# Attention of a two-layer decoder trunk: token-major projections and softmax over merged key columns, blocks outermost, in one written order with both channel mixers

## The chip, the cores and the metric

One core of a Trainium2 chip runs the whole program. The metric is the device time of one execution in microseconds, the median of several runs.

## The reference

Input x is 1024 tokens of 1024 float32 features. Layer 0 mixes tokens by a short gated convolution, layer 1 by attention; each is followed by a SwiGLU channel mixer (hidden width 2816). RMSNorm stands ahead of each of the four, a residual around it. The attention has 16 query heads of 64, 4 key/value heads, a window of 128 keys in blocks of 128 queries:

```python
q = rmsnorm(q, q_gain); k = rmsnorm(k, k_gain)          # per head of 64
scores = einsum('bnqkgd,bnskd->bnkgqs', qb, kw) * scale  # kw: previous and own block, 256 keys
dist = qi + BLOCK - kj
mask = (dist >= 0) & (dist < WINDOW) & (key_pos >= 0)
scores = where(mask, scores - slopes * dist, -inf)
p = softmax(concat([scores, sink_col]))[..., :-1]
out = einsum('bnkgqs,bnskd->bnqkgd', p, vw)
return out.reshape(bsz, s, 1024) @ w_o
```

Since the window equals the block, query i of a block sees the keys j <= i of its own block and j > i of the one before: each of the 128 columns is live in exactly one of the two.

## The kernel before, in words

Activations lie feature-major: eight tiles X of 128 features by 1024 tokens. Every product is made of three matmuls on numbers split into an upper and a lower part of fp32r (w.hi x.hi, w.hi x.lo, w.lo x.hi). The big products of the mixers use a seven-product scheme in place of eight; granule_work (L922 to L935) issues their matmuls. A class Line (L780) holds an order: work(n, f) appends TensorE work and advances a clock of planned time, at(t, f) hangs other engines' work on that clock, and run() emits all in the order of planned time under a manual schedule. The clock only sets each queue's order; on the chip every engine runs its own queue, waiting on semaphores.

The convolution layer and its channel mixer (channel_mixer, L990) are one Line, run at its end. Then attention_layer (L1524) begins anew. Keys and queries are projected with the weights stationary, so they come out feature-major, two heads to a tile (project_k L1609, the loop over i from 1 to 7 with product_by_halves L186); values are projected with tokens stationary, 256 columns at a time (project_v L1583). Sums of squares per head are matmuls with two columns (head_stats, L1536 to L1539); the inverse roots are spread to 64 columns each, transposed on TensorE and multiplied in (spread, turn_blocks L1624 to L1627, scale_rows). The softmax works on units of a tile i of two heads and a block b, 64 in all, tiles outermost. A unit's scores are four matmuls of 256 keys (scores, L1743 to L1753); VectorE adds the distance bias and finds the extreme (maxima, L1774), ScalarE exponentiates with sums (exponents, L1792), a column is blanked (blank, L1796), the weights are transposed by 128 x 128 (turn, L1798 to L1804), split (turn_hi L1811, turn_lo L1817) and multiplied with the values by up to four matmuls of 256 columns (values, L1819 to L1830). Division by the sums follows later (divide_steps, L1849), again over spread and transposed rows. A string ORDER sets the order of the steps inside a unit, and an agenda the rest:

```python
ORDER = "SPTZMEDkPHLBVOPK"
```

The output projection is split: the products over tiles 0 to 3 (L192) are threaded through the last units, those over tiles 4 to 7 are the head of the second channel mixer, which is a Line of its own (tail_part L1045, tail_item L1064, L1058 to L1060), its weights kept for both halves of the tokens. The first gate-up products come after it. SP issues the loads, GpSimd some stores.

Of the kernel before, what the change touches and what calls it, by code (L numbers as in the profile page):

```python
# [31 lines left out]
TILES = [0, 2, 1, 3, 4, 6, 5, 7]  # L32
HEADS = [2 * i + e for i in TILES for e in range(2)]
SLOPES = [2.0 ** (-8.0 * (h + 1) / NH) for h in HEADS]

# [6 lines left out]
C_INVS = C_KG + 1  # L42
C_NEGS = C_INVS + NH
C_ONES = C_NEGS + NH
C_HALF = C_ONES + 1
C_ID = C_HALF + 2
C_DIST = C_ID + P
C_END = C_DIST + 2 * P


LAG = 10

ORDER = "SPTZMEDkPHLBVOPK"


EARLY = 4
REST = 2
# [24 lines left out]
def trunk_kernel(ctx: ExitStack, tc: tile.TileContext, xT, small, w_in, w_out, w_qk, w_v, w_o, w_gu, w_dn, out):  # L82
# [136 lines left out]
    for tag in [f"G{k}" for k in range(12)]:  # L219
        slot(tag)  # L220
# [6 lines left out]
    half = cst[:, C_HALF : C_HALF + 2]  # L227
    dist = cst[:, C_DIST : C_DIST + 2 * P]

# [91 lines left out]
    def conv_layer():  # L321
# [410 lines left out]
        def lead_in(part):  # L732
# [19 lines left out]
        channel_mixer(  # L752
# [6 lines left out]
            keep_tags=None,  # L759
# [11 lines left out]
        )  # L771


    xres = [tc.dram_tile((P, T), F32, name=f"xres{m}") for m in range(NK)]
    first_sums = [[tc.dram_tile((4, P, 4 * P), F32, name=f"s1_{l}_{u}") for u in range(GROUP)] for l in range(2)]
# [214 lines left out]
    def channel_mixer(layer, next_stage, src_of, operands, raw_tags, extra_tags, keep_tags, slots, begin_with=(), first_w=None, line=None, lead_in=None):  # L990

        line = line or Line()
        at = line.at
        for t, f in begin_with:
            at(t, f)
        n_op = len(operands)
# [9 lines left out]
        kept = {}  # L1006

        def tail_weights(h, m, t):
            it = {}
            c = slice(0, n_op * P)  # L1010
            if keep_tags is None:

                def load():
                    it["w"] = Weights()
                    it["w"].load(src_of(m), 0, n_op)

                def hi():
                    it["w"].alloc()
                    it["steps"] = split_steps(it["w"].hi[:, c], it["w"].lo[:, c], it["w"].raw[:, c])
                    it["steps"][0]()  # L1020

                at(t - 14.0, load)
                at(t - 5.2, hi)
                at(t - 4.2, lambda: it["steps"][1]())
                return lambda: (it["w"].hi, it["w"].lo)
            if h == 0 and m in (first_w or ()):
                kept[m] = first_w[m]
            elif h == 0:

                def load():  # L1030
                    raw = slot("WR", (P, n_op * P), bufs=2)
                    nc.sync.dma_start(raw.rearrange("p (k c) -> p k c", c=P), src_of(m))
                    it["raw"] = raw

                at(t - 9.0, load)
                split_granule(it, lambda: it["raw"], n_op, keep_rooms[m], t - 4.0)
                kept[m] = it
            it = kept[m]
            return lambda: (it["w"][:, 0], it["w"][:, 1])

        keep_rooms = rooms(keep_tags) if keep_tags else None
# [3 lines left out]
        def tail_part(h, m, ks):  # L1045

            c = slice(h * HALF, h * HALF + HALF)
            if (h, m) not in tails:
                tails[h, m] = tail_weights(h, m, line.end), bank_at(("tail", h, m), "x", "acc")
# [14 lines left out]
        def tail_item(h, m, k0=0):  # L1064
# [5 lines left out]
            def square():  # L1070
                if m == 0:
                    state["ss", h] = slot(f"s{h}", (P, HALF))
# [47 lines left out]
        if lead_in is not None:  # L1120
            first_items = lead_in(tail_part)
# [43 lines left out]
        if not whole:  # L1165
            at(origin + 8 * tail * 0.65, load_s2)
# [1004 lines left out]
```

## Time and profile before

| | |
|---|---|
| three runs | 1949.97, 1949.94, 1949.57 us, median 1949.94 |
| profiled execution, span from first to last instruction | 1948.8 us |
| TensorE busy in it | 1937.3 us, 99% |
| VectorE, ScalarE, GpSimd busy | 71%, 44%, 13% |
| instructions | 25694 |

The time of the profiled execution is known by its span alone; what lies around it is taken as the 1.1 us between span and median. Busy shares are of the whole span; the rows below go to the stretches. A matmul's mean duration is latency in a pipeline and not its pace.

### The profile page before, as it was taken

What the parts mean: (1) busy time and instruction counts of PE and PEld (TensorE: products, weight loads), DVE (VectorE), ACT (ScalarE), POOL (GpSimd) and SP (SyncE); (2) the same over time, 40 slices, a digit from 0 to 9 for tenths busy, and PEclk for the clock granted to TensorE, in tenths of its full rate; (3) what the DMA queues carried; (4) which work ended last, traced back from release to release, by engine and by line L of the source; (5) the groups of instructions that cost most, each with busy time, mean ns of one, the idle gap of its engine ahead of it and who ended that gap; (6) DMA issues with size and microseconds to landing.
All of it is one profiled execution on the core that took longest, in us unless ns stands there. A gap on an engine that the chain in (4) does not pass through costs nothing.

```text
span 1948.8 us, 25694 instructions
## 1 busy us (share of the span) xinstructions
PE 1937.3 (99%) x9153; PEld 1618.9 (83%) x9153; DVE 1391.5 (71%) x2520; ACT 862.0 (44%) x1678; POOL 250.1 (13%) x384
## 2 busy tenths in 40 slices
PE   9999999999999999999999999999999999999999
PEld 8888888888888888888898888888888888888887
DVE  8998767877767676665645887788676767675543
ACT  5543444533333335444435777656333333344431
POOL 0000011011111110000004444410111111110000
PEclk9999999999999999999999999999999999999999
DMA  8532185244465458976300000051555565387563
GB/s 317 164 98 87 65 310 176 91 162 172 171 211 183 156 181 287 325 260 207 96 22 23 23 12 18 28 195 60 168 194 170 176 205 179 126 277 279 197 230 102
DMA packets 143170, 311.81 MB, mean 160 GB/s; under 512 B 13889, under 2 KB 53953, under 8 KB 143041
## 3 DMA queue, kind: packets, MB, share of 16 engines
q1 hardware_dynamic: 118992, 225.71, 35.0%
q0 software_dynamic: 23904, 84.42, 11.8%
q8 instruction: 72, 1.18, 0.3%
q14 instruction: 58, 0.47, 0.1%
q10 hardware_dynamic: 144, 0.03, 0.0%
HBM read 219.40 MB, written 90.70 MB: 159 GB/s over the span
## 4 chain that ended last, share of the span: by engine, by line
PE 93%; DVE 4%; ACT 1%; issue 1%; DMA 1%; ACTq 0%; DVEq 0%
PE acc L930 15%; PE acc L933 15%; PE acc L931 15%; PE P L930 9%; PE P L933 9%; PE P L931 9%; PE acc L192 5%; PE acc L169 2%; PE acc L1060 2%; PE acc L1058 2%; PE acc L1059 2%; PE P L1804 1%; PE acc L173 1%; PE P L1539 1%; PE P L1627 1%
## 5 line engine op out<-in xcount | busy, mean ns | idle before, releaser
L930 PE MATMUL acc<-XS,G 128*128 128x512 f32 x894 | 348.2, 389 | 0.0
L933 PE MATMUL acc<-XS,G 128*128 128x512 f32 x894 | 347.8, 389 | 0.0
L931 PE MATMUL acc<-XS,G 128*128 128x512 f32 x894 | 347.8, 389 | 0.0
L933 PEld LDWEIGHTS acc<-XS,G 128*128 128x128 f32 x894 | 167.8, 188 | 34.9
L931 PEld LDWEIGHTS acc<-XS,G 128*128 128x128 f32 x894 | 167.9, 188 | 34.8
L930 PEld LDWEIGHTS acc<-XS,G 128*128 128x128 f32 x894 | 167.9, 188 | 34.6
L930 PE MATMUL P<-A,G 128*128 128x512 f32 x502 | 195.3, 389 | 0.0
L931 PE MATMUL P<-A,G 128*128 128x512 f32 x502 | 195.3, 389 | 0.0
L933 PE MATMUL P<-A,G 128*128 128x512 f32 x502 | 195.3, 389 | 0.0
L930 PE MATMUL acc<-A,G 128*128 128x512 f32 x410 | 159.5, 389 | 0.0
L931 PE MATMUL acc<-A,G 128*128 128x512 f32 x410 | 159.5, 389 | 0.0
L933 PE MATMUL acc<-A,G 128*128 128x512 f32 x410 | 159.5, 389 | 0.0
L870 DVE TENSOR_TENSOR G<-WL,G 128x512 fp32r<-128x512 f32 x168 | 114.8, 684 | 53.0 <-ACT G L869 53.0
L869 ACT CAST G<-WR 128x512 fp32r<-128x512 f32 (+1 forms) x198 | 119.6, 604 | 64.4 <-PE acc L933 31.2
L870 DVE TENSOR_TENSOR G<-WR,G 128x512 fp32r<-128x512 f32 (+1 forms) x198 | 131.8, 666 | 12.4 <-ACT G L869 12.0
L869 ACT CAST G<-WH 128x512 fp32r<-128x512 f32 (+1 forms) x156 | 93.7, 600 | 77.1 <-PE acc L933 33.7
L1230 ACT ACTIVATE G<-G 128x512 f32<-128x512 f32 x88 | 55.8, 634 | 161.9 <-DVE G L1301 157.8
L869 ACT CAST G<-WL 128x512 fp32r<-128x512 f32 x168 | 103.6, 617 | 37.0 <-DVE WL L813 33.2
L930 PE MATMUL P<-XS,G 128*128 128x512 f32 x290 | 112.9, 389 | 0.1
L933 PE MATMUL P<-XS,G 128*128 128x512 f32 x290 | 112.8, 389 | 0.0
L931 PE MATMUL P<-XS,G 128*128 128x512 f32 x290 | 112.8, 389 | 0.0
L192 PE MATMUL acc<-XS,WH 128*128 128x512 f32 x320 | 110.5, 394 | 0.5 <-ACT G L1669 0.5
(328 smaller groups left out, 3991.8 us busy)
## 6 DMA issues: line engine op xcount, KB each, us to landing
G<-h SPq DMA_DIRECT2D x70, 512.0 KB, 5.5
h<-X POOLq DMA_DIRECT2D x44, 512.0 KB, 5.1
X<-in_w_dn SPq DMA_DIRECT2D x80, 256.0 KB, 3.5
s<-X POOLq DMA_DIRECT2D x40, 512.0 KB, 4.7
WR<-in_w_gu SPq DMA_DIRECT2D x36, 512.0 KB, 5.9
WH<-in_w_gu SPq DMA_DIRECT2D x36, 512.0 KB, 6.5
h<-X POOLq DMA_DIRECT2D x66, 256.0 KB, 4.1
WR<-s SPq DMA_DIRECT2D x52, 256.0 KB, 3.4
```

Of the source, the lines that this page charges most:

```text
L169: pe.matmul(ps.half(h), wh, xs[:, j, c], start=first and j == 0, stop=False)
L173: pe.matmul(ps.half(h), wl, xs[:, 0, c], start=False, stop=last)
L192: pe.matmul(ps.half(h), wp[:, kc], operands[k][:, xp, c], start=k == 0 and j == 0, stop=k == n - 1 and j == 2,)
L869: lambda: act.copy(out_hi, raw),
L870: lambda: lo_eng.tensor_tensor(out_lo, raw, plain(out_hi), ALU.subtract),
L930: pe.matmul(ps, w[:, 0, c], x[:, 0, :], start=start and e == 0, stop=False, skip_group_check=True)
L931: pe.matmul(ps, w[:, 0, c], x[:, 1, :], start=False, stop=False, skip_group_check=True)
L933: pe.matmul(ps, w[:, 1, c], x[:, 0, :], start=False, stop=last, skip_group_check=True)
L1058: pe.matmul(ps, hi[:, kc], xs[:, 0, c], start=k == 0, stop=False, skip_group_check=True)
L1059: pe.matmul(ps, hi[:, kc], xs[:, 1, c], start=False, stop=False, skip_group_check=True)
L1060: pe.matmul(ps, lo[:, kc], xs[:, 0, c], start=False, stop=k == n_op - 1, skip_group_check=True)
L1230: state["silu"] = act.activation(x, x, AF.Silu)
```

## The change

Both layers become one Line: conv_layer returns its line and mixer, and attention_layer(line, mixer) appends to it, with run() at the very end. The residual X is stored to memory (xmid) and loaded again late, and its room holds query weights. Keys and values are projected together (512 columns), queries in 16 pieces of 512 columns, all with tokens stationary, so that a head's sum of squares is a sum along the free axis (tensor_reduce on VectorE) and scaling precedes a transpose of keys and queries. Units are four heads of a block, 32, with blocks outermost. Own and previous keys' scores are merged into 128 columns by a predicated copy, a table holds the distance bias, and the minimum, the exponentials and the division (normal, on GpSimd) run over 128 columns and a sink. After the transpose the previous block's values meet all weights, and the difference of the two blocks' values meets the weights of own keys, which GpSimd selects (affine_select). The output projection is one piece after the units for each half of the tokens, its first half filling the last units; its weights are loaded for each half. The constant ones for two-column sums, the slopes and ORDER go away. A unit's steps hang on planned times from its start s:

```diff
...
+    xmid = [tc.dram_tile((P, T), F32, name=f"xmid{m}") for m in range(NK)]
     first_sums = [[tc.dram_tile((4, P, 4 * P), F32, name=f"s1_{l}_{u}") for u in range(GROUP)] for l in range(2)]
...
             at(t + 0.05, lambda: dve.tensor_tensor(X[m][:, c], get(), X[m][:, c], ALU.add))
             if k in (0, 2, 3):
                 return
+            if next_stage is not None:
+                at(t + 0.9, lambda: nc.sync.dma_start(xmid[m][:, c], X[m][:, c]))
...
+    def attention_layer(line, mixer):
+        at = line.at
+        xs = mixer.xs
+        end0 = line.end
...
+
+        def load_kv(j):
+            raw["kv", j] = slot(f"G{8 + j}", (P, 2, 2 * NKV * HD))
+            nc.sync.dma_start(raw["kv", j], w_kv[:, 2 * j : 2 * j + 2, :])
...
+        def load_q(k):
+            raw["q", k] = slot(mixer.ring.popleft())
+            nc.sync.dma_start(raw["q", k], w_q[:, k, :])
...
+            at(end0 - 28.2 + 0.4 * j, load_kv, j)
+        for k, t in enumerate((-13.6, -12.4, -11.2, -10.0, 1.3, 2.7, -4.0, -3.2)):
+            split_at(end0 + t, split_kv, k, 0.8)
+        for k, t in enumerate((-14.5, -14.4, -11.9, -9.2, -7.2, -4.5, -1.8, 0.2)):
+            at(end0 + t, load_q, k)
+        for k, t in enumerate((-2.0, -0.9, 0.2, 1.9, 3.9, 5.2, 6.6, 8.2)):
+            split_at(end0 + t, split_q, k, 1.2)
...
+        def piece(ps_of, b, k, w):
+
+            def three():
+                ps = ps_of()
+                x = xs[k]
+                t = slice(b * P, (b + 1) * P)
+                hi, lo = w()
+                pe.matmul(ps, x[:, 0, t], hi, start=k == 0, stop=False)
+                pe.matmul(ps, x[:, 0, t], lo, start=False, stop=False)
+                pe.matmul(ps, x[:, 1, t], hi, start=False, stop=k == NK - 1)
+
+            line.work(3, three)
...
+        def kv_piece(b, k):
+            piece(get_bank(kv_ps, b), b, k, lambda: (WKV[k][:, 0], WKV[k][:, 1]))
+
+        def q_piece(m, k):
+            c = slice((m % 2) * HALF, (m % 2 + 1) * HALF)
+            piece(get_bank(q_ps, m), m // 2, k, lambda: (WQ[k][0][:, c], WQ[k][1][:, c]))
...
+        def key_turn(b, c):
+            ps = KT[b, c] = bank("P3")
+            for g in (0, 1):
+                k = kd_room()[:, 2 * c + g].rearrange("p e d -> p (e d)")
+                pe.transpose(ps[:, g * P : (g + 1) * P], k, ident)
...
+        def dv_sum(b):
+            d, v, w = scratch(), plain(v_room(b)), plain(v_room(b - 1))
+            pool.tensor_tensor(d, v[:, :, 0, :], w[:, :, 0, :], ALU.subtract)
+            pool.tensor_tensor(d, d, v[:, :, 1, :], ALU.add)
...
+        def q_lo(m):
+            s = QC[m]["split"]
+            pool.tensor_tensor(s[:, :, 1, :], QC[m]["q"], s[:, :, 0, :], ALU.subtract)
+
+        def q_turn(m, g):
+            ps = QC[m]["ps"] = bank("P3")
+            s = QC[m]["split"]
+            for i in range(QUAD):
+                pe.transpose(ps[:, i * P : (i + 1) * P], s[:, QUAD * g + i].rearrange("p e d -> p (e d)"), ident)
...
+        def scores(u):
+            b, c, g = parts(u)
+            kz = key_rooms(c)[:, g]
+            S[u] = {"ps": [bank(t) for t in sc_tags]}
+            for i in range(QUAD):
+                q = Q[2 * b + c][:, g, i * P : (i + 1) * P]
+                ps = S[u]["ps"][i // 2][:, (i % 2) * 256 : (i % 2) * 256 + 256]
+                for e in (0, 1):
+                    k = kz[:, e].rearrange("p s j -> p (s j)")
+                    if b == 0:
+                        ps, k = ps[:, 0:P], k[:, 0:P]
+                    pe.matmul(ps, q, k, start=e == 0, stop=e == 1)
...
+        def merge(u, j):
+            o, p = logits(u, j)
+            dve.copy_predicated(p, own.unsqueeze(1).to_broadcast([P, 2, P]), o)
...
+        def bias(u, j):
+            b, c, g = parts(u)
+            o, p = logits(u, j)
+            h = 8 * c + QUAD * g + 2 * j
+            e = e_room(u)
+            dve.tensor_tensor(e[:, 2 * j : 2 * j + 2, 0:P], o if b == 0 else p, room["T"][:, h : h + 2, :], ALU.add)
...
+        def blank(u):
+            e = e_room(u)[:, :, 0:P]
+            pool.affine_select(e, e, [[0, QUAD], [-1, P]], ALU.is_ge, -MASKED, 0, 1)
+
+        def least(u):
+            S[u]["mx"] = slot("at_x", (P, QUAD), bufs=2)
+            dve.tensor_reduce(S[u]["mx"], e_room(u), mybir.AxisListType.X, ALU.min)
...
+        def exponents(u):
+            den = S[u]["den"] = slot("at_d", (P, QUAD), bufs=2)
+            e = e_room(u)
+            for i in range(QUAD):
+                act.activation(
+                    e[:, i], e[:, i], AF.Exp, bias=S[u]["mx"][:, i : i + 1], scale=-1.0, accum_out=den[:, i : i + 1]
+                )
...
+        def normal(u):
+            e = e_room(u)[:, :, 0:P]
+            pool.tensor_tensor(e, e, S[u]["den"].unsqueeze(2).to_broadcast([P, QUAD, P]), ALU.mult)
+
+        def turn(u):
+            ps = S[u]["pt"] = bank(pt_tag)
+            e = e_room(u)
+            for i in range(QUAD):
+                pe.transpose(ps[:, i * P : (i + 1) * P], e[:, i, 0:P], ident)
...
+        def turn_hi(u):
+            act.copy(turn_rooms()[0][:, 0], S[u]["pt"])
+
+        def turn_lo(u):
+            t = turn_rooms()[0]
+            dve.tensor_tensor(t[:, 1], S[u]["pt"], plain(t[:, 0]), ALU.subtract)
+
+        def select(u, e):
+            w, o = turn_rooms()
+            pool.affine_select(
...
+        def values(u):
+            b, c, g = parts(u)
+            kv = 2 * c + g
+            w, o = turn_rooms()
+            ps = S[u]["pv"] = bank(pv_tag)
+            flat = lambda x: x[:, kv].rearrange("p e d -> p (e d)")
+            terms = [(v_room(b - 1), w), (dv_room(b), o)] if b else [(v_room(0), w)]
+            for i, (v, t) in enumerate(terms):
+                for e in (0, 1):
+                    pe.matmul(ps, flat(v), t[:, e], start=i == 0 and e == 0, stop=i + 1 == len(terms) and e == 1)
...
+        def o_copy(u):
+            act.copy(o_rows(u), S[u]["pv"][0:HD, :])
+
+        def o_add(u):
+            o = o_rows(u)
+            dve.tensor_tensor(o, S[u]["pv"][HD:P, :], o, ALU.add)
...
+        def o_hi(n):
+            for i in range(QUAD):
+                act.copy(o_at(n, i, 0), o_room(n)[:, i * P : (i + 1) * P])
+
+        def o_lo(n):
+            for i in range(QUAD):
+                pool.tensor_tensor(o_at(n, i, 1), o_room(n)[:, i * P : (i + 1) * P], plain(o_at(n, i, 0)), ALU.subtract)
...
+            turn_query(0, 0)
+            q_piece(2, 2)
+            q_piece(2, 3)
+            turn_query(0, 1)
+
+
+            fill = []
+            for n in range(16):
+                first, second = [], []
+                if n + 2 < 16:
+                    first += [(q_piece, n + 2, k) for k in range(4, 8)]
+                if n < 12:
+                    b = n // 2 + 2
+                    first += [(kv_piece, b, 4 * (n % 2) + k) for k in (0, 1)]
+                    second += [(kv_piece, b, 4 * (n % 2) + k) for k in (2, 3)]
+                if n + 3 < 16:
+                    second += [(q_piece, n + 3, k) for k in range(4)]
...
+            def unit(u, last):
+
...
+                if u < NU:
+                    line.work(8 * (small_mm + (0.12 if b else 0.0)), scores, u)
+                    e = line.end
+                    at(s + 0.3, sink, u)
+                    for j in (0, 1):
+                        if b:
+                            at(e + 0.05 + 0.85 * j, merge, u, j)
+                        at(e + 0.5 + 0.85 * j, bias, u, j)
+                    if b == 0:
+                        at(e + 1.5, blank, u)
+                    at(e + 1.8, least, u)
+                    at(e + 2.65, exponents, u)
+                    at(e + 4.75, inverse, u)
+                    at(e + 5.0, normal, u)
+                    if g == 0:
+                        kb = (b, 1) if c == 0 else (b + 1, 0)
+                        if 0 < kb[0] < NB:
+                            turn_keys(*kb, e + 0.3, e + 2.4)
+                if 0 <= u - 2 < NU:
+                    pb = (u - 2) // 4
+                    line.work(4 if pb else 2, values, u - 2)
+                    at(line.end + 0.05, o_copy, u - 2)
+                    at(max(line.end + 0.7, s + 3.6), o_add, u - 2)
+                    if g == 1:
+                        at(s + 6.95, o_hi, n - 1)
+                        at(s + 7.9, o_lo, n - 1)
+                next_piece()
+                if 0 <= u - 1 < NU:
+                    line.work(4 * small_turn, turn, u - 1)
+                    at(line.end + 0.05, turn_hi, u - 1)
+                    at(max(line.end + 0.7, s + 4.2), turn_lo, u - 1)
+                    if u - 1 >= 4:
+                        at(line.end + 0.75, select, u - 1, 0)
+                        at(max(line.end + 1.4, s + 4.95), select, u - 1, 1)
+                if u >= NU:
+                    for _ in range(6):
+                        next_piece()
+                    return
+                for i in range(5):
+                    next_piece()
+                    if i == (1 if g == 0 else 0) and n + 1 < 16:
+                        turn_query(n + 1, g, s + 5.8)
+                if n + 2 < 16 and g == 0:
+                    m = n + 2
+                    for d, f in (
+                        (5.75, q_square),
+                        (6.35, q_sum),
+                        (7.2, q_guess),
+                        (6.8 + 3.4, q_newton),
+                        (6.8 + 5.2, q_scale),
+                        (6.8 + 6.2, q_hi),
+                        (6.8 + 7.3, q_lo),
+                    ):
+                        at(s + d, f, m)
+                if g == 1 and n < 12 and n % 2:
+                    kb = n // 2 + 2
+                    for d, f in (
+                        (3.57, kv_v_hi),
+                        (5.0, kv_v_lo),
+                        (5.7, kv_square),
+                        (6.1, kv_sum),
+                        (6.9, kv_guess),
+                        (6.8 + 3.5, kv_scale),
+                    ):
+                        at(s + d, f, kb)
+                if g == 0 and c == 1 and b + 1 < NB:
+                    at(s + 3.5, dv_sum, b + 1)
+                    at(s + 8.0, dv_hi, b + 1)
+                    at(s + 8.4, dv_lo, b + 1)
...
+            def load_again(m):
+                X[m] = slot(f"X{m}")
+                nc.sync.dma_start(X[m], xmid[m])
+
+            for u in range(NU + 2):
+                if u == 27:
+                    for m in range(NK):
+                        at(line.end + 0.6 * m, load_again, m)
+                unit(u, u == NU + 1)
...
```

## Rows read from the trace of the kernel before

**Rows 1.** The page, part 1 and the clock row of part 2

```profile
PE 1937.3 (99%) x9153; PEld 1618.9 (83%) x9153; DVE 1391.5 (71%) x2520; ACT 862.0 (44%) x1678; POOL 250.1 (13%) x384
...
PEclk9999999999999999999999999999999999999999
```

**Rows 2.** The timeline of TensorE at both ends of the stage (start us, us)

```profile
961.94 0.62 PE L169 MATMUL acc<-XS,WH 128*128 128x512 f32 x2
...
1314.99 0.39 PE L930 MATMUL acc<-XS,G 128*128 128x512 f32 x1
```

**Rows 3.** Groups of TensorE, 961.9 to 1315 (busy us, mean ns, idle before us)

```profile
L192 PE MATMUL acc<-XS,WH 128*128 128x512 f32 x320 | 110.5, 394 | 0.5 <-ACT G L1669 0.5
...
L1830 PE MATMUL P<-G,A 128*128 128x256 f32 x120 | 31.4, 282 | 0.0
...
L1804 PE MATMUL P<-cst,G 128*128 128x128 f32 x158 | 24.3, 273 | 2.7 <-DVE G L1796 2.5 <-ACT s L1792 0.2
...
L1753 PE MATMUL P<-A,G 128*128 128x256 f32 x64 | 16.6, 281 | 0.0
```

**Rows 4.** The chain that ended last, in order of time (start us, us)

```profile
986.76 1.68 PE acc L1539 x16
...
1026.03 4.53 PE acc L192 x20
...
1227.04 0.12 PE P L1829
...
1227.51 0.46 PE acc L192 x2
...
1228.91 0.44 PE P L1804 x4
```

**Rows 5.** Who TensorE waited for, 961.9 to 1315 (us, times, longest)

```profile
PE P L1804 <- DVE G L1796: 2.5, 5, 1.4
...
PE acc L169 <- ACT WH L141: 0.9, 1, 0.9
```

**Rows 6.** Groups of GpSimd, whole span

```profile
L144 POOL TENSOR_TENSOR WL<-WR,WH 128x256 fp32r<-128x256 f32 x40 | 29.3, 738 | 93.5 <-ACT WH L141 90.7 <-DVE G L1847 2.2
...
L1080 POOL DMA_DIRECT2D xres<-X x32 | 17.5, 546 | 286.8 <-DVE X L1078 286.5 <-issue 0.3
...
L1622 POOL COPY s<-den 128x512 f32<-128x512 f32 x16 | 9.8, 614 | 18.6 <-PE P L1627 14.2 <-DVE den L1856 3.9 <-POOL WL L144 0.5
L1763 POOL COPY G<-cst 128x2 f32<-128x2 f32 x42 | 7.9, 188 | 23.4 <-PE P L1804 22.9
L1941 POOL TENSOR_TENSOR XS<-G,XS 128x512 fp32r<-128x512 f32 x6 | 7.7, 1296 | 3.8 <-ACT XS L1940 3.6
```

**Rows 7.** Groups of ScalarE and VectorE, 960 to 1315

```profile
L1811 ACT CAST G<-P 128x512 fp32r<-128x512 f32 x56 | 32.6, 583 | 19.7 <-PE P L1804 19.5
...
L1846 ACT COPY G<-P 64x256 f32<-64x256 f32 x32 | 11.7, 366 | 8.8 <-PE P L1830 8.1
...
L1817 DVE TENSOR_TENSOR G<-P,G 128x512 fp32r<-128x512 f32 x56 | 38.3, 683 | 11.7 <-ACT G L1811 11.5
...
L1847 DVE TENSOR_TENSOR G<-P,G 64x256 f32<-64x256 f32 x32 | 13.6, 426 | 1.3
...
L1572 DVE SCALAR_TENSOR_TENSOR hr_y<-hr_t,hr_y 128x16 f32<-128x16 f32 x10 | 3.6, 355 | 0.3
```

**Rows 8.** Timeline of ScalarE, two exponentials with their sums (start us, us)

```profile
1106.58 0.51 ACT L1792 ACTIVATE G<-G,mx 128x256 f32<-128x256 f32 x1
...
1107.48 0.19 ACT L1792 ACTIVATION_READ_ACCUMULATOR G<-G,mx 128x1 f32 x1
```

**Rows 9.** Windows: PE, PEld, DVE, ACT, POOL busy; PEclk, DMA share, GB/s

```profile
900.00:930.00 30.00, 30.00 (x134) 24.82 (x134) 17.76 (x26) 14.31 (x23) 0.00 (x0) 1.00 0.61 194
...
1028.00:1180.00 152.00, 150.17 (x983) 132.15 (x982) 118.32 (x372) 108.93 (x329) 68.83 (x110) 1.00 0.06 20
1180.00:1224.00 44.00, 40.79 (x260) 34.88 (x261) 37.53 (x107) 31.61 (x92) 25.95 (x36) 1.00 0.04 13
```

More of the change, by code (lines that the diff above doesn't have):

```diff
@@ L29 @@
 NKV = 4
-TILES = [0, 2, 1, 3, 4, 6, 5, 7]
-HEADS = [2 * i + e for i in TILES for e in range(2)]
-SLOPES = [2.0 ** (-8.0 * (h + 1) / NH) for h in HEADS]
+SLOPES = [2.0 ** (-8.0 * (h + 1) / NH) for h in range(NH)]
+QUAD = NH // NKV
 C_GAIN = 0
@@ L81, in trunk_kernel @@
 @with_exitstack
-def trunk_kernel(ctx: ExitStack, tc: tile.TileContext, xT, small, w_in, w_out, w_qk, w_v, w_o, w_gu, w_dn, out):
+def trunk_kernel(ctx: ExitStack, tc: tile.TileContext, xT, small, table, w_in, w_out, w_kv, w_q, w_o, w_gu, w_dn, out):
     nc = tc.nc
@@ L226, in trunk_kernel @@
     ones = cst[:, C_ONES : C_ONES + 1]
-    half = cst[:, C_HALF : C_HALF + 2]
-    dist = cst[:, C_DIST : C_DIST + 2 * P]
+    own = cst[:, C_OWN : C_OWN + P].bitcast(mybir.dt.int32)
     state = {}
@@ L730, in load_again, with lead_in @@
             at(t, load)
-        def lead_in(part):
+        def lead_in(part, item):
             u = n_units - 1
@@ L750, in lead_in @@
             return {(0, 0): 4, (0, 1): 4}
-        channel_mixer(
+        mixer = channel_mixer(
             0,
@@ L1048, in tail_part @@
             if (h, m) not in tails:
-                tails[h, m] = tail_weights(h, m, line.end), bank_at(("tail", h, m), "x", "acc")
+                tag = f"P{m % 2}" if layer and h == 0 else "acc"
+                tails[h, m] = tail_weights(m, line.end), bank_at(("tail", h, m), "x", tag)
             w, get = tails[h, m]
@@ L1117, in scale @@
             dve.scalar_tensor_tensor(X[m][:, c], X[m][:, c], g, units["rows", h], ALU.mult, ALU.mult)
-        first_items = {}
-        if lead_in is not None:
-            first_items = lead_in(tail_part)
-        origin = line.end - sum(first_items.values()) * 3 * MM
-        begin1 = origin + 8 * tail
-        begin2 = origin + 16 * tail
+        first_items = lead_in(tail_part, tail_item)
+        begin1 = line.end
+        for m in range(NK):
+            n = first_items.get((0, m), 0)
+            begin1 += (n_op - n) * 3 * MM if n < n_op else 0.0
+        origin = begin1 - 8 * tail
+        begin2 = begin1 + 8 * tail
         for h in (0, 1):
             for m in range(NK):
-                tail_item(h, m, first_items.get((h, m), 0))
-        early = {(k, u): {} for k in range(3) for u in range(GROUP)}
-        extra_rooms = rooms(extra_tags)
+                if first_items.get((h, m), 0) < n_op:
+                    tail_item(h, m, first_items.get((h, m), 0))
+        whole = len(raw_tags) == GROUP
+        early = {(k, u): {} for k in range(3 if whole else 2) for u in range(GROUP)}
+        extra_rooms = rooms(extra_tags) if whole else None
         pairs = [{} for u in range(GROUP)]
-        whole = len(raw_tags) == GROUP
         def first_raw(u, k):
@@ L2149, in _layout @@
     }
-_NAMES = ["xT", "small", "w_in", "w_out", "w_qk", "w_v", "w_o", "w_gu", "w_dn"]
+_NAMES = ["xT", "small", "table", "w_in", "w_out", "w_kv", "w_q", "w_o", "w_gu", "w_dn"]
 def kernel(**inputs):
```

899 lines of the change are left out of this document (349 added, 550 removed).

## The prediction

> **What bounds the kernel now.** First the page's engine shares and clock row [rows 1]: TensorE is busy for 1937.3 of a span of 1948.8 us, at full granted clock in every slice. What the other engines do counts only where TensorE waits, so the change is worth TensorE time removed, plus waits removed, less waits added. Second, the order of TensorE's instructions at both ends of what is rewritten [rows 2]: the first key projection starts at 961.94, the first gate-up product of the second channel mixer at 1314.99. The attention, its projections and the output projection (I call this stretch the stage) take 353.05 us; of the rest nothing changes on TensorE. Third, the groups of that stretch [rows 3]: the reader sees 512-column matmuls, 256-column ones (scores L1753, values L1830, and the value projection) and two sorts of tiny ones, transposes (L1804, and L1627 which spreads row scales) and the two-column squares of L1539. Their means (273 to 394 ns) are pipelined latencies; the pace is in the chain of waits [rows 4]: 4.53 us for twenty 512s, 0.2265 each; 0.47 for four 256s, 0.1175 each; 0.44 for four transposes, 0.110 each; 1.68 for sixteen two-column ones, 0.105 each. A two-column matmul costs almost what a transpose does, and half of a 512.
>
> With the counts that the code gives and the groups bear out, the stage is 864 x 0.2265 = 195.7, 688 x 0.1175 = 80.8, 388 transposes x 0.110 = 42.7, 184 tiny x 0.105 = 19.3: 338.5 us. The remaining 14.6 of 353.05 are no work: TensorE's waits sum to 5.8 us in seven groups, the largest 2.5 (transposes of the softmax behind the blanking of a column) [rows 5]; the other 8.8 are slower issue where kinds are mixed.
>
> **The change on TensorE.** Keys and values: 8 blocks x 8 k x 3 = 192 of 512 in place of 96 of 512 and 192 of 256, the same columns. Queries 384 and output projection 384 of 512, as before. Values: 28 units x 4 + 4 x 2 = 120 of 512 in place of 240 of 256. Scores: 28 units x 8 = 224 of 256, and 32 of 128 columns, a form that the trace lacks: not under a transpose's 0.110 (same columns, same weight load), not over a 512's 0.2265; I take 0.110, the nearest, and the other end adds 3.7. Transposes: the weights need 32 x 4 = 128 in place of 240, since own and previous keys are merged into 128 columns; queries 128 and keys 32 replace the 144 that spread row scales; four of the norm stay. Tiny: the 160 of L1539 go (the squares are now summed along the free axis by VectorE), 24 stay. Sum: 1080 x 0.2265 = 244.6, 224 x 0.1175 = 26.3, 324 x 0.110 = 35.6, 24 x 0.105 = 2.5: 309.0. **29.5 us less work**, 16.8 of it from L1539.
>
> [...]
>
> **What the other engines must do per unit.** A unit is four heads of one block; there are 32, and in the steady part TensorE works for 18 x 0.2265 (six pieces of projections) + 8 x 0.1175 + 4 x 0.2265 + 9 x 0.110 = 6.92 us in each. Here is what two units ask of the others.
> GpSimd [rows 6]: normalising 2 x 1.29, lower part of the queries 1.29, of the outputs 4 x 0.46 (on the line through 0.738 at 256 and 1.29 at 512), sinks 2 x 0.19, value differences half of 4 x 0.738: 7.6, so 3.8 a unit, plus two masks of 128x512 (affine_select). That instruction is not in the trace: it is bounded below by the copy of 512, 0.614, one operand in, one out, and above by two passes of a two-operand 512, 2.58. I take the copy, since it too reads one operand: 5.0 of 6.92.
> ScalarE [rows 7]: eight exponentials with their sums, at most 0.55 each (two of 256 columns took 1.09 in the timeline [rows 8]; these have 129): 4.4; eight copies or squares of 512 at 0.58, five of 128 to 256 at 0.37, two small ones at no more than that, and half of the keys' and values' four of 256 and two small: 1.1. At most 12.7 of 13.84.
> VectorE [rows 7]: four merges and four biases of 256 at 0.43, two minima, two lower parts, two sums, one squares' sum and one scaling of 512 at 0.68, keys 0.43, six small ones at no more than 0.36, and half of the keys' and values' four of 256 and four small, 1.6: at most 13.1 of 13.84. The merge (predicated copy) and the reduction are not in the trace; a merge lies between 0.43 and twice that (1.7 more in two units, 14.8, 0.9 over TensorE in each of 14 pairs, 13 in all, which the range holds), and I take the plain price, the row that it is nearest to, being one pass over as many columns; the reduction the same way.
> So TensorE stays the bound, with three neighbours at 72 to 95%, the last two as upper bounds. What the order leaves for latency: from the end of a unit's scores, merges and biases 1.7, minimum 0.7, exponentials 2.2, inverse 0.36, normalising 1.3 end at 7.2 after the unit's start; its transposes stand behind the next unit's scores, two-units-old values and one piece, at 9.45. From there 0.44, upper part 0.58, lower part 0.68, second mask 0.61 end at 11.8; the values read at 14.8. Some 2 to 3 us of slack at both places, which a late queue eats.
>
> **Stalls that I allow.** Of the same three engines under load the old trace shows two rates: in 1028 to 1180 TensorE is idle 1.8 of 152 us (1.2%), in 1180 to 1224, with VectorE at 85%, 3.2 of 44 (7.3%) [rows 9]. On 221 us of units that is 2.7 to 16; I take 6. Slower issue scales with tiny matmuls, 348 for 572: 8.8 becomes 5.4. Together 11.4 for 14.6.
> The seam: before, the mixer's order ended and the attention's began with loads, splits and 0.9 us of wait [rows 5]; now projections follow at once. The new transfers there, on SP's queue, are keys' and values' weights 2 MB, queries' 4 MB, table 1 MB, and the residual's last 1 MB of stores, over some 35 us: 230 GB/s beside the products' own loads; at 900 to 930 the queues carried 194 at a share of 0.61 [rows 9], about 318 at full share, so it fits, with 5 us in the range if it comes late. The residual's reload (8 x 512 KB) lies behind the last query products and in front of the output projection's adds; at 318 GB/s it takes 13 us, and an add comes every 5.4. Cost 0, hidden by the units. The output projection's weights are loaded and split twice (8 more of 512 KB and of 1024 columns on ScalarE and VectorE), one per 5.4 us of products: hidden by them. Its first half's ends move into the last units and behind them: per 5.4 us one add, one square and one sum of 512 (VectorE 1.4, ScalarE 0.6) and one store that GpSimd issues in 0.55 [rows 6]; by then query and key work is gone, so they fit. The second mixer loses one granule prepared early; its loads stand 20 us ahead: 0.
>
> **Sum.** On the span: 1948.8 - 29.5 - 14.6 + 11.4 = 1916.1. The runs' median, 1949.94, lies 1.1 above the span (launch and end around it), so **1917.2**.
>
> **Rivals.**
> (1) GpSimd becomes the bound; this one ends slower. Place: the two masks per unit between transposes and values, from unit 4 on, in 28 units. At two passes (2.58) GpSimd needs 3.8 + 5.16 = 8.96, 2.04 over TensorE's 6.92: 28 x 2.04 = 57, so 1974. It is slower than before from 32.7 / 28 = 1.17 a unit on, a mask of 2.15 us. For it: no row has this instruction, and a two-operand 512 already takes 1.29. Against: the one-operand copy takes half of that. [...] Chance 0.10.
> (2) A mask between 1.6 and 2.15: at 1.9 GpSimd needs 7.6, 28 x 0.68 = 19: 1936. Same rows, milder. Chance 0.14.
> (3) The written order makes TensorE wait once a unit, for the transposes or the values, since VectorE and ScalarE are near full and every queue is in order: 1 us a unit, 28: 1945. For it: the loss of 7.3% where VectorE was at 85%. Against: the slack above. Chance 0.08.
>
> **How the numbers follow.** My forecast, TensorE-bound with small stalls, has 0.68: 1908 (hardly a stall, 3 us in all) to 1927 (stalls at the 7% rate, or a late start). The range 1908 to 1941 takes in (2), up to a mask of 2.0, and part of (3). 0.2% (3.9 us, about what a measurement of this kernel can tell from no change) is reached by all but (1) and the upper end of (2) and (3): faster 0.88, same 0.02, slower 0.10.
>
> **What would show it.** Right: the stage at 312 to 330 us; no matmul of two columns there but the token means; GpSimd's masks near 0.6 to 1.3 us and GpSimd under 80% in the units; units 7.0 to 7.3 us apart. Wrong: TensorE's waits led by the values' matmuls behind GpSimd (rivals 1 and 2) or by transposes behind VectorE or ScalarE (3), a wait at the first projections behind DMA, or 128-column score matmuls at over 0.2 us.

## The result and the profile after

The changed kernel takes 1955.01 us (median of eight runs, 1954.33 to 1955.64) against 1949.91 (eight runs, 1949.57 to 1952.61): ratio 1.0025, interval 1.0014 to 1.0035. It is slower by 5 us where 33 less were forecast. The profiled execution has a span of 1952.6 us, 3.8 more than before.

Part 1 of the page of the changed kernel, and the clock row of part 2, look as before [rows 1]:

```profile
PE 1935.1 (99%) x8681; PEld 1580.7 (81%) x8681; DVE 1384.0 (71%) x2357; ACT 855.7 (44%) x1703; POOL 280.6 (14%) x442
...
PEclk9999999999999999999999999999999999999999
```

TensorE is again busy 99% of the span at full clock, with 472 fewer matmuls. So first the stage's ends, as [rows 2] gave them. Timeline of TensorE in the changed kernel (start us, us):

```profile
978.56 0.39 PE L1590 MATMUL P<-WR,XS 128*128 128x512 f32 x1
...
1305.84 0.39 PE L918 MATMUL acc<-A,G 128*128 128x512 f32 x1
```

The stage takes 327.3 us in place of 353.05: **25.8 us were saved where the change was made.** But it begins 16.6 us later, and what follows it takes 646.8 in place of 633.8. So **29.6 us were lost outside the stage, where the change leaves TensorE's products as they were**: 4197 matmuls of 512 columns ahead of the stage and 2772 behind it in both kernels. 29.6 - 25.8 is the 3.8 of the spans. One thing did move: eight one-column matmuls (token means) that stood in the stage now stand ahead of it. Before, in the stage:

```profile
962.85 0.95 PE L280 MATMUL P<-cst,s 128*128 128x1 f32 x8
```

At the 0.105 us that [rows 4] give for a two-column matmul that is 0.84 of the 16.6.

How an untouched stretch loses time is seen in a window that holds nothing but mixer products, 100 to 500 us (columns: PE, PEld, DVE, ACT, POOL busy with counts; granted clock, DMA share, GB/s). Before:

```profile
100.00:500.00 400.00, 399.94 (x1777) 331.11 (x1776) 314.16 (x497) 163.98 (x279) 27.40 (x45) 1.00 0.42 145
```

After:

```profile
100.00:500.00 400.00, 399.94 (x1752) 326.63 (x1751) 308.85 (x486) 161.70 (x274) 25.83 (x42) 1.00 0.41 144
```

TensorE is as busy, its clock is as full, it waits for nothing: and it gets 25 matmuls less through, 1.4%. In the order of TensorE's starts the mixers before have a matmul every 226 or 227 ns throughout. After, that holds for three of every eight granules (a granule is twelve matmuls on one weight slot) whose weights lie in the slots G0 to G7; in the other five they start 231 to 235 ns apart, 233 on average. In the timeline of slow granules of the changed kernel, the ninth matmul after another starts 2.09 us later, 0.232 each (before: 0.2265 [rows 4]):

```profile
104.69 0.40 PE L919 MATMUL acc<-XS,G 128*128 128x512 f32 x1
...
106.78 0.40 PE L919 MATMUL acc<-XS,G 128*128 128x512 f32 x1
```

Three and five of eight is how the ring of weight slots G0 to G7 divides at G2. The change has one line that the diff above leaves out, and that the prediction did not speak of: slot G2 is made eight floats wider, since it also holds the 4 x 129 weights of two units.

```diff
     for tag in [f"G{k}" for k in range(12)]:
-        slot(tag)
+        slot(tag, (P, D + 8) if tag == "G2" else (P, D))
```

Slots are laid out in the order of their first use, XS0 to XS7, A0 to A5, WR, WH, WL, G0 to G11, s0, s1, X0 to X7, all of 2048 bytes a partition or a multiple. So before, any two of them stood a multiple of 2048 bytes apart; after, G3 and all behind it stand 32 bytes off that.

Inside the stage most of the forecast's prices were right. GpSimd's and VectorE's groups of the changed kernel from 978 to 1306 us:

```profile
L1864 POOL TENSOR_SCALAR_AFFINE_SELECT G<-G 128x512 fp32r<-128x512 f32 x56 | 35.7, 643 | 59.3 <-ACT G L1856 33.5 <-DVE G L1860 25.7
L1842 POOL TENSOR_TENSOR G<-G,at_d 128x512 f32<-128x512 f32 x32 | 34.2, 1068 | 17.4 <-DVE at_d L1838 17.0 <-POOL G L1864 0.2
```

```profile
L1807 DVE COPY_PREDICATED acc<-cst,acc 128x256 f32<-128x256 int32 x56 | 23.6, 421 | 11.1 <-PE acc L1797 11.1
L858 DVE TENSOR_TENSOR WL<-WR,WH 128x1024 fp32r<-128x1024 f32 x16 | 23.1, 1446 | 5.3 <-ACT WH L857 5.2
L1827 DVE TENSOR_REDUCE at_x<-G 128x4 f32<-128x516 f32 x32 | 22.1, 691 | 8.7 <-POOL G L1823 5.9
```

The mask takes 0.643 us, the merge 0.421, the reduction 0.691. What TensorE waits for there, as in [rows 5] (us, times, longest):

```profile
PE P L1762 <- DVE G L1705: 4.7, 1, 4.7
PE P L1762 <- DVE at_t L1625: 1.8, 1, 1.8
PE acc L1848 <- POOL G L1842: 1.4, 1, 1.4
PE P L1590 <- DVE G L1683: 1.3, 1, 1.3
PE P L1696 <- ACT G L1767: 1.2, 2, 0.7
```

One wait stands out. The timeline around it (start us, us):

```profile
1207.56 3.64 DVE L858 TENSOR_TENSOR WL<-WR,WH 128x1024 fp32r<-128x1024 f32 x1 [2.04 <-ACT WH L857]
1207.83 1.69 POOL L1914 TENSOR_TENSOR XS<-s,XS 128x128 fp32r<-128x128 f32 x4
...
1209.49 0.62 POOL L1864 TENSOR_SCALAR_AFFINE_SELECT G<-G 128x512 fp32r<-128x512 f32 x1
...
1213.03 0.47 DVE L1705 SCALAR_TENSOR_TENSOR G<-P,qkg,G 128x256 fp32r<-128x256 f32 x1
...
1213.65 1.08 PE L1762 MATMUL P<-cst,G 128*128 128x128 f32 x4 [4.68 <-DVE G L1705]
```

and its windows, columns as above:

```profile
1208.00:1212.00 4.00, 0.97 (x5) 0.47 (x3) 3.96 (x4) 0.84 (x2) 2.11 (x5) 1.00 0.01 2
1212.00:1214.00 2.00, 0.35 (x2) 0.38 (x3) 1.87 (x4) 0.85 (x5) 0.00 (x0) 0.80 0.79 262
1214.00:1216.00 2.00, 2.00 (x8) 1.71 (x7) 0.92 (x2) 1.36 (x6) 0.64 (x1) 0.50 0.00 0
1216.00:1218.00 2.00, 2.00 (x11) 1.63 (x10) 1.33 (x3) 0.63 (x1) 1.09 (x2) 0.84 0.00 0
```

The low part of an output weight (L858) waits 2.0 us at the head of VectorE's queue for ScalarE, then takes 3.64 us in place of 1.22 (the median of its group of 16). The keys' low part (L1705) stands behind it, and the bank that TensorE's next transposes (L1762) need is free only after that. TensorE waits 4.7 us; late in that wait the granted clock falls from 1.00 to 0.50, and by the three last windows, taken as mixtures of these two, it stays there for 3.4 us (0.8, 2.0 and 0.6).

### The profile page after: what moved, and what is told of

It reads as the page before. It is cut to its first block, busy times and chain, and to the rows that moved or that the text cites. A ratio compares the mean times of both kernels' runs of the same rounds, so it can differ in the third digit from the quotient of the medians.

```text
span 1952.6 us, 24622 instructions
## 1 busy us (share of the span) xinstructions
PE 1935.1 (99%) x8681; PEld 1580.7 (81%) x8681; DVE 1384.0 (71%) x2357; ACT 855.7 (44%) x1703; POOL 280.6 (14%) x442
## 4 chain that ended last, share of the span: by engine, by line
PE 94%; DVE 3%; ACT 1%; issue 1%; POOL 0%; DMA 0%; SPq 0%; DVEq 0%; POOLq 0%; ACTq 0%
PE acc L921 16%; PE acc L918 16%; PE acc L919 16%; PE P L921 9%; PE P L918 9%; PE P L919 9%; PE acc L1027 2%; PE acc L1025 2%; PE acc L1026 2%; PE P L1590 2%; PE P L1592 2%; PE P L1591 2%; PE acc L1797 1%; PE acc L157 1%; PE acc L1883 1%
## 5 line engine op out<-in xcount | busy, mean ns | idle before, releaser
L918 PE MATMUL acc<-XS,G 128*128 128x512 f32 x880 | 346.1, 393 | 0.0
L919 PEld LDWEIGHTS acc<-XS,G 128*128 128x128 f32 x880 | 165.3, 188 | 38.5
L921 PEld LDWEIGHTS acc<-XS,G 128*128 128x128 f32 x880 | 165.2, 188 | 38.0
L918 PEld LDWEIGHTS acc<-XS,G 128*128 128x128 f32 x880 | 165.3, 188 | 37.9
L918 PE MATMUL P<-A,G 128*128 128x512 f32 x476 | 187.1, 393 | 0.6 <-DVE G L1234 0.6
L921 PE MATMUL P<-A,G 128*128 128x512 f32 x476 | 187.4, 394 | 0.0
L919 PE MATMUL P<-A,G 128*128 128x512 f32 x476 | 187.0, 393 | 0.0
L921 PE MATMUL acc<-A,G 128*128 128x512 f32 x440 | 173.4, 394 | 0.0
L918 PE MATMUL acc<-A,G 128*128 128x512 f32 x440 | 173.2, 394 | 0.0
L919 PE MATMUL acc<-A,G 128*128 128x512 f32 x440 | 173.0, 393 | 0.0
L858 DVE TENSOR_TENSOR G<-WL,G 128x512 fp32r<-128x512 f32 x168 | 114.9, 685 | 56.6 <-ACT G L857 56.6
L858 DVE TENSOR_TENSOR G<-WR,G 128x512 fp32r<-128x512 f32 (+1 forms) x200 | 133.3, 666 | 12.0 <-ACT G L857 11.2
L921 PE MATMUL P<-XS,G 128*128 128x512 f32 x316 | 124.4, 394 | 0.0
L919 PE MATMUL P<-XS,G 128*128 128x512 f32 x316 | 124.2, 393 | 0.0
L918 PE MATMUL P<-XS,G 128*128 128x512 f32 x316 | 124.2, 393 | 0.0
L858 DVE TENSOR_TENSOR G<-WH,G 128x512 fp32r<-128x512 f32 (+1 forms) x158 | 104.4, 661 | 5.4 <-ACT G L857 5.1
```

The source lines that it names most:

```text
L858: lambda: lo_eng.tensor_tensor(out_lo, raw, plain(out_hi), ALU.subtract),
L918: pe.matmul(ps, w[:, 0, c], x[:, 0, :], start=start and e == 0, stop=False, skip_group_check=True)
L919: pe.matmul(ps, w[:, 0, c], x[:, 1, :], start=False, stop=False, skip_group_check=True)
L921: pe.matmul(ps, w[:, 1, c], x[:, 0, :], start=False, stop=last, skip_group_check=True)
```

## Experiments: the lost 29.6 us

**Sixteen floats.** Theory A: it is the address. Rival B: the written order and its waits; rival C: other traffic.

```diff
-        slot(tag, (P, D + 8) if tag == "G2" else (P, D))
+        slot(tag, (P, D + 16) if tag == "G2" else (P, D))
```

> The changed kernel with its slot G2 sixteen floats wider instead of eight; every instruction and their order as before. What this moves: the slots G3 to G11, s0, s1 and X0 to X7 stand 32 bytes off a multiple of 64 bytes in the changed kernel, and at multiples of 64 in the kernel before and in this one. Theory A (address): the 512-column products whose weights lie in a slot that is 32 bytes off issue every 231 to 235 ns instead of 226 to 227, and that alone is what slowed the mixers outside the attention stage. Then all products outside the stage go back to 226 or 227 ns, the stretch from 40 us to the stage takes 921 to 924 us (938.7 now), what follows the stage 629 to 632 (642.6 now), the stage 320 to 327, and the whole is near 1926 us (1920 to 1932). Rival B (the one written order and its waits slow the products): nothing moves, 1955 within 3. Rival C (the transfers or the other engines' traffic slow them): as B.

1956.61 us, ratio 1.0033 (1.0020 to 1.0045). The window of this kernel:

```profile
100.00:500.00 400.00, 399.94 (x1750) 326.39 (x1749) 308.43 (x484) 161.82 (x274) 25.83 (x42) 1.00 0.41 144
```

Nothing came back, the same five of eight granules are slow. As written, theory A fell here; B and C stood.

**The kernel before, with addresses alone changed.** A 32-byte tile that stood behind X7 is first used elsewhere; every engine's instructions and their order stay. First behind G2:

```diff
     for tag in [f"G{k}" for k in range(12)]:
-        slot(tag)
+        _ = slot(tag), tag == "G2" and slot("r", (P, NB))
```

> The kernel before with its small tile r (32 bytes) placed behind G2 instead of behind X7: G3 to G11, s0, s1 and X0 to X7 go 32 bytes off a multiple of 64; instructions and order stay. Theory A (address of the weights): the same five of eight granules of the mixers go to 231 to 235 ns, some 29 us outside the stage and 0 to 8 us in it: 1979 us (1972 to 1988). Rival B (the written order): 1950 within 3. Rival D (the address matters for the operand that streams through, not for the weights): 1950 within 5, since the streamed slots XS and A are not moved.

1977.53 us, ratio 1.0140 (1.0126 to 1.0154):

```profile
100.00:500.00 400.00, 399.94 (x1752) 326.61 (x1751) 308.82 (x485) 161.81 (x274) 25.83 (x42) 1.00 0.41 144
```

The old kernel gets the changed kernel's 1752 and loses 27.3 us (1950.21 for the kernel before beside these runs). So B and C are out: address alone does it. Then ahead of XS0, with a second such tile behind A5:

```diff
+    _ = slot("r", (P, NB)), [pair_slot(tag) for tag in [f"XS{k}" for k in range(NK)] + [f"A{k}" for k in range(6)]]
+    _ = slot("rs_m", (P, NB))
```

> The kernel before with r placed ahead of XS0 and rs_m behind A5: only XS0 to XS7 and A0 to A5, which the products stream through, go 32 bytes off a multiple of 64; the weights' slots stay at multiples of 64. Theory A (weights): 1950 to 1953, the paces of the mixers unchanged at 226 or 227 ns. Rival D (streamed operand): every product of the mixers goes to 231 to 235 ns, 40 us and more: 1985 or above. Rival B: 1950 within 3.

1995.98 us, ratio 1.0234 (1.0221 to 1.0248), every granule slow:

```profile
100.00:500.00 400.00, 400.00 (x1730) 322.76 (x1729) 305.85 (x479) 160.88 (x272) 25.83 (x42) 1.00 0.41 141
```

This is rival D's number, though D had just failed: with weights moved it is slow, with the streamed operand moved it is slow too. 27.3 is five eighths of 43.7, near the 45.8 lost here, where all eight slots are off. What these two, the changed kernel and the one with sixteen floats share is a difference between the two addresses (32, 32, 32 and 64 bytes) that is no multiple of some larger power of two. That is theory A2.

**All slots equal again; all moved together; other distances.** G2 first used behind X7, with the order of instructions untouched:

```diff
-    for tag in [f"G{k}" for k in range(12)]:
-        slot(tag, (P, D + 8) if tag == "G2" else (P, D))
+    for tag in [f"G{k}" for k in range(12) if k != 2]:
+        slot(tag)
...
-    X = [slot(f"X{k}") for k in range(NK)]
+    X, _ = [slot(f"X{k}") for k in range(NK)], slot("G2", (P, D + 8))
```

> The changed kernel with its wider slot G2 (1032 floats) allocated behind X7 instead of between G1 and G3; instructions and order as in the changed kernel. Theory A2 (relative address): what failed with sixteen floats was the modulus: a 512-column product issues every 226 or 227 ns only where the weights' slot and the streamed slot have the same address modulo some power of two above 64 (in the kernel before all slots are multiples of 4096 or 2048 bytes apart), and every 231 to 236 ns otherwise. Here all slots are multiples of 2048 bytes apart again: the products outside the stage go back to 226 or 227 ns, the stretch from 40 us to the stage takes 921 to 924 us, what follows the stage 629 to 632, the stage 320 to 327: 1926 us (1920 to 1932). Rival B (the written order, transfers or other engines slow the products): 1955 within 3.

**1927.35 us**, ratio 0.9881 (0.9866 to 0.9896), as A2 had it:

```profile
100.00:500.00 400.00, 399.94 (x1776) 331.12 (x1775) 314.37 (x497) 163.95 (x279) 27.44 (x45) 1.00 0.42 145
```

The stage begins at 962.78 and ends at 1291.00:

```profile
962.78 0.39 PE L1590 MATMUL P<-WR,XS 128*128 128x512 f32 x1
...
1291.00 0.39 PE L918 MATMUL acc<-A,G 128*128 128x512 f32 x1
```

So 15.8 of the 16.6 us ahead of the stage are back, and 634.8 follow it. Then the kernel before with the small tile ahead of XS0 only, so that weights and streamed operand move 32 bytes together:

> The kernel before with r placed ahead of XS0, so that every slot of the weights and of the streamed operand goes 32 bytes up together. Theory A2 (relative address): weights and streamed operand still agree, 1950 within 3. Rival A3 (absolute address: a slot has to stand where it stands in the kernel before, 64 modulo 128): every product of the mixers slow, 1985 to 2000. Rival B: 1950 within 3.

1950.27 us, ratio 1.0000 (0.9990 to 1.0009):

```profile
100.00:500.00 400.00, 399.94 (x1776) 331.10 (x1775) 314.28 (x496) 164.11 (x279) 27.47 (x45) 1.00 0.42 145
```

So a move of both doesn't matter; how far the one operand stands from the other does. Last, the changed kernel with G2 wider by 32, 64 and 128 floats (D + 8 replaced), which puts G3 and the rest 128, 256 and 512 bytes off:

> The changed kernel with G2 32 floats wider: G3 to G11, s0, s1 and X0 to X7 stand 128 bytes off from where they would be with equal slots, so weights and streamed slots agree modulo 128 and no further. Theory A2 with a modulus of 128: as with G2 last, 1926 us (1920 to 1932). With a modulus of 256 or more: 1953 to 1958, as with sixteen floats. Rival B: 1955 within 3.

> The changed kernel with G2 64 floats wider: weights' slots G3 to G11 stand 256 bytes off from the streamed slots' address modulo 4096. If the modulus is 256: 1927 within 3, all products outside the stage at 226 or 227 ns. If it is larger: 1950 to 1957, and five of eight granules slow.

> The changed kernel with G2 128 floats wider: 512 bytes off. If the modulus is 256 or 512: 1927 within 3. If it is 1024 or more: 1950 to 1957.

128 bytes: 1953.12 us, ratio 1.0015 (1.0005 to 1.0024). 256: 1927.47, 0.9881 (0.9865 to 0.9898). 512: 1927.06, 0.9881 (0.9867 to 0.9896). Their windows, in that order:

```profile
100.00:500.00 400.00, 399.94 (x1754) 327.55 (x1753) 309.29 (x485) 161.75 (x274) 25.83 (x42) 1.00 0.42 144
```

```profile
100.00:500.00 400.00, 399.94 (x1776) 331.08 (x1775) 314.35 (x497) 163.83 (x279) 27.25 (x45) 1.00 0.42 145
```

```profile
100.00:500.00 400.00, 399.94 (x1776) 331.08 (x1775) 314.32 (x497) 163.83 (x279) 27.27 (x45) 1.00 0.42 145
```

The step lies between 128 and 256 bytes: at differences of 32, 64 and 128 the window holds 1730 to 1754 matmuls, at 256, 512 and multiples of 2048 it holds 1776 or 1777.

## Experiments: the wait in the stage

**Low parts 1.6 us later**, on the kernel with sixteen floats:

```diff
-            at(t - 4.2, lambda: it["steps"][1]())
+            at(t - (2.6 if layer and m < 4 else 4.2), lambda: it["steps"][1]())
```

> The kernel with sixteen floats, and the low parts of the output weights for row blocks 0 to 3 (VectorE, 128x1024) placed 1.6 us later on VectorE, behind the merges and biases of a unit; nothing else moves. In the changed kernel the one of 1207.6 us held VectorE's queue for 2.0 us of waiting and 3.6 us of work, and TensorE then waited 4.7 us for the keys' low part and fell to the lower clock level for some 3 us. Theory: that place costs 5 to 8 us, and 3 to 7 of them come back against the kernel with sixteen floats (near 1921). Rival: the wait moves on (the low parts come late for the output products, or another VectorE step is held), and the time stays within 2 us of the kernel with sixteen floats.

1954.76 us (1951.53 to 1955.52), ratio 1.0018 (1.0009 to 1.0028), 1.9 under sixteen floats but with overlapping intervals: inconclusive by time. By the waits the mechanism held in part:

```profile
PE P L1762 <- DVE G L1705: 2.8, 1, 2.8
```

VectorE no longer idles ahead of the low part, but that still takes 3.37 us with the keys' low part behind it. In the eleven runs the time goes with the mean granted clock: 1951.5 and 1951.6 us at 1.000, 1952.9 to 1953.3 at 0.999, 1954.8 to 1955.5 at 0.998. The profiled execution, one of the last kind, is granted 0.99 from 1208 to 1212 us, 0.50 from 1212 to 1214 and 0.66 from 1214 to 1216, which makes 3.4 us at 0.50 there. The two runs at 1.000 are 5 us under sixteen floats, inside the 3 to 7 expected.

**3.0 us later, with G2 last** (2.6 replaced by 1.2), so that the keys' low part goes first:

> G2 last, and the low parts of the output weights for row blocks 0 to 3 placed 3.0 us later on VectorE, behind the keys' low part too. With sixteen floats, 1.6 us later gave 1.9 us and left a wait of 2.8 us, because the 128x1024 step took 3.4 us where GpSimd worked beside it and the keys' low part stood behind it. Theory: with the keys' low part ahead of it that wait of TensorE goes (under 0.5 us) and with it the stretch at the lower clock level: 4 to 6 us less than G2 last alone, near 1921 (1916 to 1925). Rival: the output products then wait for their low parts instead, and it is within 1.5 us of G2 last alone.

1925.18 us (1923.89 to 1925.90), ratio 0.9870 (0.9854 to 0.9887): 2.2 under G2 last and not 4 to 6, with a mean granted clock of 1.000 in the profiled execution (0.998 with G2 last). The wait of 4.7 is gone, and others have come:

```profile
PE P L1027 <- DVE WL L858: 2.3, 2, 1.3
...
PE acc L1027 <- DVE WL L858: 1.4, 2, 0.7
```

The output products wait for low parts that had not been in anybody's way: too much was moved. **Row block 2 alone**, later; and in another run earlier, both its halves:

```diff
-            at(t - 4.2, lambda: it["steps"][1]())
+            at(t - (1.2 if layer and len(tails) == 2 else 4.2), lambda: it["steps"][1]())
```

> G2 last, and of the output weights' low parts only the one for row block 2 placed 3.0 us later on VectorE (it was the one of 3.6 us; with four row blocks moved in both halves, row block 0 and two blocks of the second half came late and cost 2.4 us of new waits). Theory: the 4.7 us wait for the keys' low part goes as with the four moved, the new waits go but for some 1 us for row block 2 itself: 1923 us (1920 to 1924.5). Rival: the new waits come from GpSimd's traffic, wherever the step stands: 1925 or above.

```diff
+            at(t - (7.2 if layer and len(tails) == 2 else 5.2), hi)
+            at(t - (6.2 if layer and len(tails) == 2 else 4.2), lambda: it["steps"][1]())
```

> G2 last, and for row block 2 alone both halves of the split of its weights 2.0 us earlier: the high part on ScalarE ahead of the queries' copy, the low part on VectorE ahead of one merge. Theory (the low part held VectorE because ScalarE's high part was late and GpSimd then worked beside it): the low part no longer waits 2.0 us, starts before GpSimd's long steps and takes under 2 us; the wait for the keys' low part shrinks to under 2 us, and 2 to 4 us come back: 1924.5 us (1923 to 1926). Rival: the queries' copy, 1.05 us later on ScalarE, makes TensorE wait at the next turn of the queries or keys, and it stays at 1927 within 1.

Later: **1921.60 us** (1921.47 to 1921.90), ratio 0.9853 (0.9839 to 0.9868), the fastest version here. Its waits in the stage, and a window at the place:

```profile
PE P L1762 <- DVE at_t L1625: 1.8, 1, 1.8
PE acc L1848 <- POOL G L1842: 1.5, 1, 1.5
PE P L1027 <- DVE WL L858: 1.3, 1, 1.3
```

```profile
1198.00:1200.00 2.00, 2.00 (x13) 1.65 (x12) 1.93 (x5) 0.58 (x1) 0.71 (x2) 1.00 0.76 291
```

The 4.7 us wait is out, the low part itself makes TensorE wait 1.3, as expected, and the clock stays at 1.00. In the kernel with G2 last the same window shows 0.50 and 8 matmuls for 13:

```profile
1198.00:1200.00 2.00, 2.00 (x8) 1.71 (x7) 0.96 (x2) 1.40 (x6) 0.64 (x1) 0.50 0.00 0
```

Earlier: 1921.95 us (1921.82 to 1922.08), ratio 0.9855 (0.9840 to 0.9870), better than its expected 1923 to 1926. The low part took 2.06 us; the queries' copy, now behind on ScalarE, costs what the rival had said, but only 0.9 us more (2.1 for 1.2):

```profile
PE P L1696 <- ACT G L1767: 2.1, 2, 1.4
...
PE P L1762 <- DVE G L1705: 0.6, 1, 0.6
```

Two opposite moves gain the same 5.4 to 5.8 us. What they have in common is that the low part no longer keeps VectorE from the keys just when TensorE needs them; in neither does the clock fall (1.000 in all eight runs).

## Why the prediction was wrong

- **The step that failed** is half a sentence ahead of the sum: "of the rest nothing changes on TensorE". Its products don't change; their pace does. Outside the stage 29.6 us are lost, 27.8 of which come back with the slots; by time it is 27.7 (1955.01 to 1927.35). The other 1.8 are the eight means and the 0.9 named below. None of the rivals had it: all three lay within the stage, which at 327.3 us was inside the 312 to 330 given as a sign of being right.
- With that undone the kernel lands at 1927.35, within 1908 to 1941, 10.1 above the forecast: 7.8 in the stage (328.2 for 320.4), 0.8 ahead of it (the eight means, counted within the stage by the forecast), 0.9 behind it, 0.5 around the span. Of the 0.9, 0.8 are put down to one wait of TensorE for VectorE in the second mixer (L918 for L1234: 0.6 us in the changed kernel, 0.8 with row block 2 later), which the kernel before doesn't have; why it came was not tested.
- **Work on TensorE, 309.0 us**, held: the trace has every matmul that was counted, with 16 of the 24 tiny ones still in the stage, and at the same prices that is 308.25 there. The 32 scores of 128 columns, a form that no row had, came 0.11 us apart, as taken. The chain of waits of the changed kernel (start us, us) has eight scores of 256 in 0.95 us and four transposes in 0.44:

```profile
1061.28 0.95 PE acc L1797 x8
...
1120.23 0.44 PE acc L1848 x4
```

  Steady units come 6.89 and 7.15 us apart in turn, 14.04 a pair; the forecast had 13.84 of work.
- **Stalls were too small**: 19.0 us beyond work in the changed kernel, 20.0 with G2 last, where 11.4 stood. In the changed kernel TensorE's waits (those above and two short ones) make 11.1 of that where 6 stood; the rest, 7.9 for 5.4, is slower issue and the 3.4 us at a clock of 0.50. One event makes most of the difference, worth 5.75 us by the run that removes it, wait and clock together. It sits in a step that was costed at nothing: the output weights' second splitting, "hidden" by 5.4 us of products. The cover was TensorE's; what was full was VectorE's queue, and who stood behind the waiting step was not asked. Two smaller waits go with the same splitting. The 1.8 us for L1625 shrinks to 0.2 where the four low parts stand 1.6 us later. The 1.4 us for GpSimd's L1842 follows the low part of 1238.70, shown in the last section.
- **Rivals 1 and 2 fall.** The mask takes 0.643 us, 0.03 over the price taken, far from 1.6 or 2.15. GpSimd was busy 97.5 us of 1028 to 1180, 64%.
- **Rival 3 falls**: no wait once a unit; the waits above come once or twice in all. The merge and the reduction cost what was taken for them.
- **The seam** cost 0 as taken: the first projections wait for no load. With G2 last they start 0.84 us later than before the change, which is what the eight means ahead of them take.

## What to carry to other kernels

Where a change adds, widens or drops a buffer, ask how far every later one moves against those that TensorE reads beside it: here the mixers' products ran 3% slower where weights and streamed operand stood 32 bytes off a multiple of 2048, and the odd-sized tile at the end of the layout gave 27.7 us back. First compare the number of matmuls in a window that the change doesn't touch (1777 and 1752 here); busy share and clock (399.94 of 400 us and 1.00 in both) showed nothing of this loss. A split or copy that seems free because its consumer is late can be paid by whoever stands behind it in its engine's queue: here a step of 3.64 us on VectorE, and 4.7 us of waiting on TensorE.

## What the runs showed of the hardware

- In the mixers a 512-column matmul started every 226 or 227 ns where the two operands' addresses differed by a multiple of 2048 bytes, and every 233 ns on average at a difference of 32, a pace 3% lower. By the matmuls in the window of 100 to 500 us, 256 and 512 bytes go with the first (1776 in each), 64 and 128 with the second (1750 and 1754, for 1752 in the changed kernel). With both operands moved 32 bytes together it was 1776. So the pace was not independent of how the two operands lie to each other; what makes it so, and why the step lies between 128 and 256, stays open. So does why the stage suffered little or nothing: its query weights in X0 to X7 were off from XS as well, with the roles exchanged (tokens stationary, weights streamed), yet it took 327.3 us, and 328.2 with G2 last. The first twelve query products with weights in X started 234 ns apart in the changed kernel (993.10 to 995.67 us) and 226 with G2 last (977.33 to 979.82); but the next six, whose weights lie in A and had not moved against XS, also started 232 ns apart in the one and 226 in the other.
- VectorE's 128x1024 subtraction took 3.64 us in place of 1.22 where GpSimd had begun ahead of it and went from instruction to instruction until 1210.11: it ended 1.08 us after that, as if it had stood still until then. With the low parts 1.6 us later it took 3.37, GpSimd went on until 1209.85, and it ended 1.08 us after that again. In the one place below it began first, and GpSimd's step was the longer one. This product of GpSimd (1.04 us otherwise) ended 0.90 us after VectorE's step:

```profile
1238.70 1.19 DVE L858 TENSOR_TENSOR WL<-WR,WH 128x1024 fp32r<-128x1024 f32 x1
...
1238.93 1.86 POOL L1842 TENSOR_TENSOR G<-G,at_d 128x512 f32<-128x512 f32 x1 [0.79 <-DVE at_d L1838]
```

  What holds the one up beside the other is not shown: no run here took GpSimd's work away.
- TensorE's granted clock fell to 0.50 late in the wait of 4.7 us and stayed there for 3.4 us in the changed kernel. With G2 last three windows of 2 us from 1196 us on were granted 0.61, 0.50 and 0.50, some 5.6 us at 0.50; a window of 2 us then held 8 matmuls for 13. With the wait gone, in the two runs that moved row block 2, it stayed at 1.00.
